# Key and value pages grouped by eight, state updates on the full array, own values in the values' bank, and another order of the mLSTM weight tiles

## The chip, the cores and the metric

One core of one Trainium2 chip runs the whole kernel in one launch. The metric is the device time of the execution in microseconds (us), as the median over the runs.

## The reference

One inference step of a two-layer decoder trunk, for a prompt of 256 tokens and for 8 sample sequences of 8 tokens each (320 token columns in all, model width 2048). Layer 0 projects the input and feeds two groups of heads:

- MoBA attention, 8 heads of 128. The prompt attends causally. Each sample sequence has a paged cache of 2048 keys and values (16 pages of 128); per query the three blocks of 256 keys with the largest `q . mean(k)` are kept, and the new keys (the "own" ones) are added.
- mLSTM matrix memory, 4 heads of 256, with a state `C` (256 x 256) per sample and head, read and replaced.

```python
k_mean = jnp.mean(kb.astype(f32), axis=2)
gate = jnp.einsum('bshd,bnhd->bhsn', q.astype(f32), k_mean)
_, idx = lax.top_k(gate, n_sel)
...
o = jnp.einsum('bhqk,bkhd->bhqd', p[..., :ko], v_own.astype(f32))
o = o + jnp.einsum('bhqnk,bhqnkd->bhqd', p[..., ko:].reshape(bsz, nh, nq, n_sel, kb), v_sel.astype(f32))
...
c_new = decay[..., None, None] * c + jnp.einsum('bhsd,bhse->bhde', kc * wk[..., None], vc)
```

Both groups are gated and go through one output projection and a LayerNorm. Layer 1 is a gated short convolution with four input projections of 2048 and one output projection, again with a LayerNorm. All weights are float32.

## The kernel before, in words

Activations stand transposed (channels on partitions, 320 tokens free). Every weight is cut into tiles of 2048 x 128, and each into two halves of 128 x 1024 floats (512 KB): an *item*. To keep float32 accuracy each half is split into a high and a low part, `sh` by ACT and `sl` by DVE (`split`, line 201), and PE makes three products for each 128 rows (`lin_pe`, line 230): 24 matmuls of 320 columns per half. The bank of the result has the name `lin`.

The cache is read whole. It has 256 *page items* of two 256 KB pages each, grouped into four units (`Unit`, line 441) of four sequences and four heads: 32 key items (`k_item`, line 496) and 32 value items (`v_item`, line 585) per unit. A key item is 4 matmuls, a value item 8; each has a 128-row, 32-column part of the array as its tile, so that four run side by side (`kv<-raw,qp` and `kv<-raw,PT` in the profile). Eight key items give two blocks of scores, eight value items one group `g` of a unit.

All items pass through one ring: SP loads item after item, in the order of the list `items`, into 9 buffers `raw` (`RAW`, line 1376; `ahead`, line 1382). The buffer of a page item is free when PE has used it; that of a weight half when it is split, into one of 4 pairs `sh`/`sl` (`HL`). Before each page load SP reads the page's number from the page table (`page`, line 451). In the list, pages and weight halves are mixed evenly (lines 1154 to 1159): 256 page items to 132 weight halves, that is two page items, then one half, and so on. The last four halves (`TAIL`) come behind all pages.

Everything else (softmax, prompt attention, the mLSTM heads, LayerNorm, the new states) is written as generators in four chains A, B, C, E (`Chain`, line 97), of which one step each is set behind every second 128-row group of a weight half and behind each item (`stages`, line 1414), when a planner (`Plan`, line 69) that counts made-up times per engine finds that its inputs are due. `ahead(must, limit)` decides when a weight half is split: at once if its place is below `must`, otherwise when the planner takes it as loaded. `must` is `i + 2`, the item behind the present one.

The parts that the change touches: `softmax` scales the own scores (line 559); `v_out_task` (line 614) makes the own values' product with four matmuls into bank `mA`, copies it with ACT, and adds it to the transposed output; `post_qm`, `post_km`, `post_vm` (lines 741 to 797) take the mLSTM tiles of a head in the order q, k, v, and the head's generator `mlstm_head` (line 816) is queued behind v; there `states(p)` (line 868) reads two of the eight state tiles `cb` with 4 matmuls, once for each of three groups of tokens and once more for the last (`mC<-cb,qw`). The tiles `cb` have 4 buffers, filled by POOL's DMAs. In `new_states` (line 1233), which runs in layer 1, each of 32 state updates is two matmuls with only 32 rows (`mC<-Xl`), one `scalar_tensor_tensor` of DVE (`xr`), and a load and a store of 256 KB on POOL's queue.

Of the kernel before, what the change touches and what calls it, by code (L numbers as in the profile page):

```python
# [53 lines left out]
TAIL = 4  # L54
SLACK = -0.3
# [94 lines left out]
def trunk_kernel(ctx, tc, x_in, kc, vc, pages, cst_in, seg_in, hot_in, small_in, c0_in, n0_in, w_in,  # L150
# [371 lines left out]
    def softmax(u):  # L522
# [36 lines left out]
        dve.tensor_scalar(S[:, 2048:2112], S[:, 2048:2112], u.rinv[:, 0:1], None, op0=OP.mult)  # L559
# [25 lines left out]
    def v_item(u, g, b4, pp):  # L585
        def pre():
            if (g, b4, pp) == (0, 0, 0):
                u.v = kv_bank()
            if (b4, pp) == (0, 0):
                A.until(f"pt{u.n}.{g}")  # L590
            if (g, b4, pp) == (3, 3, 1):
                C.until(f"post{cga[4 * u.half + 3]}")
                B.until(f"v{4 * u.half + 3}")
                A.until(f"po{u.n}")

        def pe(raw, between):
            r = raw.rearrange("p (g f) -> p g f", g=2)
            for n in range(2):
                for j in range(4):
                    mm(u.v[32 * j:32 * j + 32, 128 * b4:128 * b4 + 128],  # L600
                       lhsT=u.PT[g][:, 2 * pp + n, 32 * j:32 * j + 32], rhs=r[:, n, 128 * j:128 * j + 128], tiles=4,
                       start=g == b4 == pp == n == 0, stop=g == 3 and pp == n == 1, skip_group_check=True)
            if b4 == 3 and pp == 1:
                pv_groups[0] += 1

        def post():
            if u.n:
                A.until(f"out{u.n - 1}")
            O = pa_.tile([128, 4, 128], F32, name="O", tag="O")
            act(O, u.v.rearrange("p (b d) -> p b d", b=4), AF.Identity, scale=u.rinv[:, 0:1])  # L610
            A.add_urgent(f"out{u.n}", v_out_task(u, O))
        return Item(v_load(u, b4, 2 * g + pp), pe, post if (g, b4, pp) == (3, 3, 1) else None, pre=pre, split=False)

    def v_out_task(u, O):

        yield
        t = a_bank()
        for j in range(4):
            h = 4 * u.half + j
            mm(t[:, 32 * j:32 * j + 32], lhsT=vs[:, h * 128:h * 128 + 128], rhs=u.PO[:, 32 * j:32 * j + 32],  # L620
               start=True, stop=True)
        yield HOLD
        own = pa_.tile([128, 4, 32], F32, name="u", tag="u")
        act(own, t[:, :128].rearrange("p (j c) -> p j c", j=4), AF.Copy)
        yield
        t = a_bank()
        for b in range(4):
            transpose(t[:, b * 128:b * 128 + 128], O[:, b, :], ident)
        yield HOLD
        o4 = own.rearrange("p j (b q) -> p j b q", b=4)  # L630
        dve.tensor_tensor(o4, _free(t, 0, [[32, 4], [136, 4], [1, 8]]), o4, op=OP.add)
        m = M[:, 4 * u.half:4 * u.half + 4, T + 32 * u.quad:T + 32 * u.quad + 32]
        dve.tensor_tensor(m, m, own, op=OP.mult)
        yield
# [106 lines left out]
    def post_qm(hd, kt):  # L741
        def f(p):
            if kt == 0:
                if hd >= 1:
                    B.until(f"read{hd - 1}")
                qm[hd] = ml.p.tile([128, 2, N], F32, name="qm", tag="qm")
            act(qm[hd][:, kt, :], p, AF.Copy)
        return f

    def post_km(hd, kt):  # L750
        def f(p):
            if kt == 0:
                km[hd] = ml.p.tile([128, 2, N], F32, name="km", tag="km")
                if hd == 0:
                    c_load(4)
            act(km[hd][:, kt, :], p, AF.Copy, scale=1.0 / 16)
            B.add(f"k{hd}.{kt}", k_natural(hd, kt))
# [5 lines left out]
    def c_load(count):  # L763
        for _ in range(count):
            if ml.c_next < BH * NB:
                c = ml.p.tile([128, 512], F32, name="cb", tag="cb", bufs=4)
                nc.gpsimd.dma_start(c, c0_in[ml.c_next // NB, C_ORDER[ml.c_next % NB]])
                ml.cb.append(c)
                ml.c_next += 1
# [20 lines left out]
    def post_vm(hd, kt):  # L790
        def f(p):
# [3 lines left out]
            if kt == 1:  # L795
                B.add(f"mlstm{hd}", mlstm_head(hd))
# [19 lines left out]
    def mlstm_head(hd):  # L816
# [42 lines left out]
        yield HOLD  # L859
        dve.tensor_tensor(dt[:, 0:384], t[:, 0:384], dt[:, 0:384], op=OP.mult)  # L860
# [3 lines left out]
        sm = P2.tile([128, 64], F32, name="sm", tag="sm")  # L864
        dve.memset(sm[:, 32:48], 1.0)
# [12 lines left out]
        for j, (c, n) in enumerate(TOK):  # L878
            states(j)
# [7 lines left out]
            else:  # L887
                yield
# [243 lines left out]
    for step in MLSTM_ORDER:  # L1132
        for n, c in enumerate(take(6 if step[0] == "h" else 4)):
            i = int(step[1])
            if step[0] == "h":
                lh += lin_items(Lin(c, (post_qm, post_km, post_vm)[n // 2](i, n % 2)))
            else:
# [16 lines left out]
    for n, it in enumerate(order):  # L1154
        items.append(it)
        goal = 2 + (free - 2) * (n + 1) // len(order)
# [27 lines left out]
    def to_out_even():  # L1184
# [10 lines left out]
        for u in X2["U"]:  # L1195
            nc.gpsimd.memset(u[:, 0:2], 0.0)
        X2["nc"] = p.tile([128, 16, 18], F32, name="ncv")
# [35 lines left out]
    def new_states():  # L1233


# [17 lines left out]
        for n in range(BH * NB):  # L1253
# [160 lines left out]
    def stages():  # L1414
# [3 lines left out]
        ahead(i + 2, i + AHEAD)  # L1418
        plan.t = t

# [12 lines left out]
    while i < len(items):  # L1433
# [20 lines left out]
        if it.split:  # L1454
            for n in range(g):
                ended[used_up + n] = end
            ahead(i + 2, i + AHEAD)
            used_up += g
        else:
            freed[i] = end  # L1460
            ahead(i + 2, i + AHEAD)
# [153 lines left out]
```

## Time and profile before

| what | value |
| --- | --- |
| median of 3 runs | 1518.67 us (1513.85 to 1520.48) |
| profiled execution | 1513.19 us, span 1511.4 us |
| PE matmuls busy | 1488.2 us, 98% of the span |
| DVE, ACT, POOL busy | 777.3 us, 593.2 us, 140.8 us |
| TensorE clock, mean granted | 0.996 |
| data moved | 356 MB, mean 236 GB/s |

The span is the time from the first to the last instruction; 1.8 us of the execution lie outside it. Matmuls are pipelined, so that the busy share of PE says little by itself: two neighbours overlap, and what one costs is the distance between their starts. The pages are used from 44 us to 768 us, layer 0's output projection follows until about 905 us, then layer 1.

### The profile page before, as it was taken

Reading aid. Unit: us, or ns where it says so; the run is one execution under the profiler, and the core shown is the slowest. Engines: PE = TensorE matmul, PEld = TensorE weight load, DVE = VectorE, ACT = ScalarE, POOL = GpSimd, SP = SyncE. Lnnn points to the kernel's source line nnn. Section 1 sums busy time; section 2 is a strip of 40 time slices with the busy share of each in tenths; the row PEclk is TensorE's granted clock in tenths of the full one; section 3 lists DMA queues with packets and bytes.
Section 4 is the critical chain, followed back from the end, with each engine's and each line's share of the span. In section 5 each row is a group of like instructions: output and inputs, shape, how many; then the busy total and the mean of one; then the engine's idle time right before and its main releaser. Section 6 shows DMA issues by size and latency. Waiting matters only on the chain.

```text
span 1511.4 us, 31909 instructions
## 1 busy us (share of the span) xinstructions
PE 1488.2 (98%) x11983; PEld 1370.5 (91%) x11983; DVE 777.3 (51%) x1304; ACT 593.2 (39%) x1097; POOL 140.8 (9%) x263
## 2 busy tenths in 40 slices
PE   9999999999999999999999999999999999999998
PEld 9887889988888788899899999999999999999997
DVE  5224334333343423623456766666666666666665
ACT  5224435433334333433354444333333333333444
POOL 0100000010111101101001015313110000000000
PEclk9999999999999999999999999999999999999999
DMA  9999889989989789989864557767555444444422
GB/s 337 294 310 308 298 291 322 317 290 324 310 290 294 268 288 316 311 290 304 291 234 160 190 159 218 217 215 223 203 198 184 141 140 162 145 140 158 153 70 70
DMA packets 148652, 356.42 MB, mean 236 GB/s; under 512 B 24325, under 2 KB 30726, under 8 KB 148498
## 3 DMA queue, kind: packets, MB, share of 16 engines
q1 hardware_dynamic: 126338, 317.26, 61.9%
q0 software_dynamic: 22160, 37.13, 8.3%
q8 instruction: 94, 1.54, 0.4%
q14 instruction: 60, 0.49, 0.1%
HBM read 337.31 MB, written 16.98 MB: 234 GB/s over the span
## 4 chain that ended last, share of the span: by engine, by line
PE 81%; issue 8%; DMA 5%; SPq 2%; DVE 2%; ACT 1%; POOL 1%; ACTq 0%; POOLq 0%; DVEq 0%
PE lin L163 69%; PE kv L163 7%; DMA raw<-w_all 3%; PE mC L163 2%; PE mB L163 2%; DMA bt<-rel 1%; SPq L452 1%; ACT sh L85 1%; PE mB L168 1%; DVE sl L85 1%; DMA cb<-c 0%; SPq L467 0%; PE mA L163 0%; DVE M L85 0%; SPq L459 0%
## 5 line engine op out<-in xcount | busy, mean ns | idle before, releaser
L85 DVE TENSOR_TENSOR sl<-raw,sh 128x1024 fp32r<-128x1024 f32 (+1 forms) x341 | 412.6, 1215 | 527.1 <-ACT sh L85 525.9
L85 ACT ACTIVATE sh<-raw 128x1024 fp32r<-128x1024 f32 (+1 forms) x341 | 355.8, 1048 | 475.9 <-DMA raw<-w_all 255.4
L163 PE MATMUL lin<-Xh,sh 128*128 128x320 f32 x1648 | 532.7, 323 | 1.8 <-DVE sg L85 1.8
L163 PE MATMUL lin<-Xh,sl 128*128 128x320 f32 x1648 | 510.0, 309 | 0.0
L163 PE MATMUL lin<-Xl,sh 128*128 128x320 f32 x1648 | 509.8, 309 | 0.0
L163 PEld LDWEIGHTS lin<-Xh,sh 128*128 128x128 f32 x1648 | 310.5, 188 | 42.3 <-issue 31.3
L163 PE MATMUL lin<-X2h,sh 128*128 128x322 f32 x1024 | 321.9, 314 | 0.0
L163 PE MATMUL lin<-X2l,sh 128*128 128x322 f32 x1024 | 318.0, 311 | 0.0
L163 PE MATMUL lin<-X2h,sl 128*128 128x322 f32 x1024 | 317.8, 310 | 0.0
L163 PEld LDWEIGHTS lin<-Xl,sh 128*128 128x128 f32 x1648 | 311.0, 189 | 0.6
L163 PEld LDWEIGHTS lin<-Xh,sl 128*128 128x128 f32 x1648 | 310.3, 188 | 0.0
L163 PEld LDWEIGHTS lin<-X2h,sh 128*128 128x128 f32 x1024 | 192.9, 188 | 4.4
L163 PEld LDWEIGHTS lin<-X2l,sh 128*128 128x128 f32 x1024 | 193.7, 189 | 0.1
L163 PEld LDWEIGHTS lin<-X2h,sl 128*128 128x128 f32 x1024 | 192.6, 188 | 0.0
L163 PE MATMUL kv<-raw,qp 128*32 128x256 f32 x1024 | 71.0, 388 | 6.2 <-ACT vstage L85 3.3
L163 PE MATMUL kv<-raw,PT 128*32 128x128 f32 x2048 | 71.1, 277 | 0.0
L163 PEld LDWEIGHTS kv<-raw,PT 128*32 128x32 f32 x2048 | 51.8, 110 | 14.1 <-issue 11.8
L163 PEld LDWEIGHTS kv<-raw,qp 128*32 128x32 f32 x1024 | 26.3, 109 | 29.5 <-issue 15.1
L85 DVE SCALAR_TENSOR_TENSOR xr<-xr,dec,mC 128x512 f32<-128x512 f32 x32 | 23.9, 746 | 36.6 <-PE mC L163 31.7
L85 ACT ACTIVATE sg<-sg 128x320 f32<-128x320 f32 x72 | 33.8, 469 | 14.2 <-DVE sg L85 12.5
L85 ACT ACTIVATE lnq<-M 128x320 f32<-128x320 f32 x30 | 14.2, 472 | 59.0 <-DVE M L85 59.0
L85 DVE SCALAR_TENSOR_TENSOR z<-lnc,ze,lin 128x320 f32<-128x320 f32 x64 | 34.7, 542 | 2.9 <-ACT ze L85 2.9
(308 smaller groups left out, 1021.5 us busy)
## 6 DMA issues: line engine op xcount, KB each, us to landing
raw<-w_all SPq DMA_DIRECT2D x335, 512.0 KB, 4.7
raw<-kc SPq DMA_DIRECT2D x256, 256.0 KB, 4.3
raw<-vc SPq DMA_DIRECT2D x256, 256.0 KB, 4.5
cb<-c POOLq DMA_DIRECT2D x32, 256.0 KB, 5.8
xr<-c POOLq DMA_DIRECT2D x32, 256.0 KB, 4.8
cs_o<-xr POOLq DMA_DIRECT2D x32, 256.0 KB, 2.8
xr<-x_in POOLq DMA_DIRECT2D x16, 160.0 KB, 3.4
y_o<-M SPq DMA_DIRECT2D x16, 160.0 KB, 1.8
```

The source lines that it names most:

```text
L85: return fn(out, *a, **k)
L163: nc.tensor.matmul(out, lhsT=lhsT, rhs=rhs, **k)
L168: nc.tensor.transpose(out, in_, identity)
L452: return nc.sync.value_load(pt[0:1, b * NPG + j:b * NPG + j + 1], min_val=0, max_val=NPOOL - 1)
```

## The change

Six edits and a small one, the core of the diff below.

1. `BUNCH = 8`: the list `items` takes eight page items in a row, then the four (sometimes five) weight halves that belong to them.
2. `soon()` replaces `i + 2` as the place below which halves are split at once: it looks ahead over items worth 4 us in the planner's counting (3.5 for a half, 0.5 for a page item). `c_load` adds 0.77 to the planner's DMA time for each tile.
3. `new_states`: ACT copies a block of 128 rows of keys times a column that is 1 in the 32 rows of the sample and 0 elsewhere (tile `kb`), and the two matmuls then have all 128 rows.
4. Own values: four matmuls with 64 rows, 32 columns and 512 elements (`kv<-vs,PO`) add them in the bank of the values, behind the last page of a unit; the four matmuls into `mA`, the copy, one addition and the scaling in `softmax` go.
5. The mLSTM tiles come in the order v, k, q; `mlstm_head` is queued behind q, and the wait for the reads of the head before is at k.
6. In `mlstm_head`, `states(0)` and `states(1)` stand together, and `states(2)` and `states(3)`.
7. A `memset` of DVE moves ahead of two operations.

```diff
-        dve.tensor_scalar(S[:, 2048:2112], S[:, 2048:2112], u.rinv[:, 0:1], None, op0=OP.mult)
...
+            if (g, b4, pp) == (3, 3, 1):
+                for j in range(4):
+                    h = 4 * u.half + j
+                    mm(u.v[32 * j:32 * j + 32, :], lhsT=u.PO[:, 32 * j:32 * j + 32],
+                       rhs=vs[:, None, h * 128:h * 128 + 128].to_broadcast([64, 4, 128]), tiles=4,
+                       start=False, stop=True, skip_group_check=True)
...
-        for j in range(4):
-            h = 4 * u.half + j
-            mm(t[:, 32 * j:32 * j + 32], lhsT=vs[:, h * 128:h * 128 + 128], rhs=u.PO[:, 32 * j:32 * j + 32],
-               start=True, stop=True)
-        yield HOLD
-        own = pa_.tile([128, 4, 32], F32, name="u", tag="u")
-        act(own, t[:, :128].rearrange("p (j c) -> p j c", j=4), AF.Copy)
...
     def post_km(hd, kt):
         def f(p):
             if kt == 0:
+                if hd >= 1:
+                    B.until(f"read{hd - 1}")
...
+                plan.dma += 0.77
...
         for j, (c, n) in enumerate(TOK):
-            states(j)
+            if j == 0:
+                states(0)
+                states(1)
...
-                yield
+                states(2)
                 states(3)
...
+            c = take(6)
+            for n in (4, 5, 2, 3, 0, 1):
+                lh += lin_items(Lin(c[n], (post_qm, post_km, post_vm)[n // 2](i, n % 2)))
...
-    for n, it in enumerate(order):
-        items.append(it)
-        goal = 2 + (free - 2) * (n + 1) // len(order)
+    for n in range(0, len(order), BUNCH):
+        items += order[n:n + BUNCH]
+        goal = 2 + (free - 2) * (n + BUNCH) // len(order)
...
-            for _ in range(6):
+            for _ in range(2):
                 yield
             kS, vS = kv[hd]
-            r = slice(32 * (b % 4), 32 * (b % 4) + 32)
+            kb = late.tile([128, DK], F32R, name="kb", tag="kb")
+            act(kb, kS[:, b // 4, :].bitcast(F32), AF.Identity, scale=X2["rows"][:, b % 4:b % 4 + 1])
+            yield
+            yield
             u = c_bank()
             for kt in range(2):
-                mm(u[:, kt * 256:kt * 256 + 256], lhsT=kS[r, b // 4, kt * 128:kt * 128 + 128], rhs=vS[r, b // 4, :],
+                mm(u[:, kt * 256:kt * 256 + 256], lhsT=kb[:, kt * 128:kt * 128 + 128], rhs=vS[:, b // 4, :],
                    start=True, stop=True)
...
+    def soon():
+
+        n, t = i + 1, 0.0
+        while n < len(items) and t < 4.0:
+            t += 3.5 if items[n].split else 0.5
+            n += 1
+        return n
...
-            ahead(i + 2, i + AHEAD)
+            ahead(soon(), i + AHEAD)
```

What stands on the engines differs at three places. The line numbers of the change are one higher there.

PE, before, at the first key pages of unit 0 (the three `lin` names are the three products of a weight half, of which 24 stand between two visits of the pages):

```order
L163 MATMUL lin<-Xl,sh 128x320
L163 MATMUL lin<-Xh,sl 128x320
L163 MATMUL kv<-raw,qp_102 32x256 x8
L163 MATMUL lin<-Xh,sh 128x320
L163 MATMUL lin<-Xl,sh 128x320
```

PE, with the change, at the same place (96 `lin` matmuls stand between two such visits):

```order
L164 MATMUL lin<-Xl,sh 128x320
L164 MATMUL lin<-Xh,sl 128x320
L164 MATMUL kv<-raw,qp_102 32x256 x32
L164 MATMUL lin<-Xh,sh 128x320
L164 MATMUL lin<-Xl,sh 128x320
```

Eight matmuls (two page items) became 32 (eight items). Over the whole order, matmuls of pages stand in 143 unbroken runs before and in 52 with the change: 32 bunches, and 20 places where a chain's matmuls fall into one.

SP, before, at the loads for unit 0 (each page load has a read of the page table, `TENSOR_LOAD pt`, and two register instructions ahead of it; four of them stand between two loads of weight halves, `raw<-w_all`):

```order
L459 DMA raw<-kc 128x512
L225 DMA raw<-w_all 128x1024
L452 TENSOR_LOAD pt
L452 ISA x2
L459 ISA
L459 DMA raw<-kc 128x512
```

SP, with the change, at the same place (16 page loads stand between two such groups):

```order
L460 DMA raw<-kc 128x512
L226 DMA raw<-w_all 128x1024 x4
L453 TENSOR_LOAD pt
L453 ISA x2
L460 ISA
L460 DMA raw<-kc 128x512
```

Four weight halves are now loaded in a row, behind sixteen page loads with their reads of the page table; their number is the same.

PE, before, at the reads of the old states in mLSTM head 0 (the first of four such visits):

```order
L163 MATMUL lin<-Xh,sl 128x320
L163 MATMUL mC<-cb,qw 32x256 x4
L163 MATMUL mB<-vn,dt 128x257
L163 MATMUL lin<-Xh,sh 128x320
L163 MATMUL lin<-Xl,sh 128x320
```

PE, with the change, at the same place (the first of two visits):

```order
L164 MATMUL lin<-Xh,sl 128x320
L164 MATMUL mC<-cb,qw 32x256 x8
L164 MATMUL mB<-vn,dt 128x257
L169 MATMUL mA<-cst,S 128x128 x4
L164 MATMUL lin<-Xh,sh 128x320
```

All four buffers of `cb` are read at once, and the second visit, 42 to 54 `lin` matmuls later, needs all four filled anew.

## Rows read from the trace of the kernel before

**Rows 1.** The page, parts 1 and 2 (40 slices of 37.8 us).
```profile
PE 1488.2 (98%) x11983; PEld 1370.5 (91%) x11983; DVE 777.3 (51%) x1304; ACT 593.2 (39%) x1097; POOL 140.8 (9%) x263
...
PEclk9999999999999999999999999999999999999999
DMA  9999889989989789989864557767555444444422
GB/s 337 294 310 308 298 291 322 317 290 324 310 290 294 268 288 316 311 290 304 291 234 160 190 159 218 217 215 223 203 198 184 141 140 162 145 140 158 153 70 70
```

**Rows 2.** Busy time by stretch: all pages; then three stretches behind them.
```profile
core 0: us, PE busy (x) PEld busy (x) DVE busy (x) ACT busy (x) POOL busy (x), PEclk, DMA share, GB/s
44.00:768.00 724.00, 710.46 (x6830) 607.41 (x6823) 267.37 (x527) 274.92 (x576) 58.29 (x109) 0.99 0.90 302
768.00:905.00 137.00, 135.22 (x916) 133.99 (x914) 91.05 (x143) 64.94 (x105) 12.96 (x25) 1.00 0.52 176
905.00:1152.00 247.00, 247.00 (x1596) 236.35 (x1594) 165.20 (x247) 89.16 (x154) 66.86 (x120) 1.00 0.66 210
1152.00:1499.00 347.00, 346.96 (x2340) 345.80 (x2340) 221.39 (x336) 134.31 (x222) 1.08 (x2) 1.00 0.39 130
```

**Rows 3.** Timeline of PE around two key page items (start us, us, engine).
```profile
309.61 0.31 PE L163 MATMUL lin<-Xh,sh 128*128 128x320 f32 x1
...
310.34 0.31 PE L163 MATMUL lin<-Xh,sl 128*128 128x320 f32 x1
310.58 1.07 PE L163 MATMUL kv<-raw,qp 128*32 128x256 f32 x16
311.58 0.42 PE L163 MATMUL lin<-Xh,sh 128*128 128x320 f32 x1
311.84 0.31 PE L163 MATMUL lin<-Xl,sh 128*128 128x320 f32 x1
```

**Rows 4.** The same around a single key page item.
```profile
383.77 0.31 PE L163 MATMUL lin<-Xh,sl 128*128 128x320 f32 x1
384.01 0.64 PE L163 MATMUL kv<-raw,qp 128*32 128x256 f32 x8
...
384.84 0.31 PE L163 MATMUL lin<-Xl,sh 128*128 128x320 f32 x1
```

**Rows 5.** Timeline of SP's queue.
```profile
370.47 0.37 SPq L225 DMA_DIRECT2D raw<-w_all  x1
371.68 3.69 SPq L467 DMA_DIRECT2D raw<-vc  x4
375.47 0.37 SPq L225 DMA_DIRECT2D raw<-w_all  x1
```

**Rows 6.** DMA issues: median us to landing, first of 44 to 110 us.
```profile
raw<-w_all SPq DMA_DIRECT2D x13, 512.0 KB, 5.3
```

**Rows 7.** The same of 850 to 1400 us.
```profile
raw<-w_all SPq DMA_DIRECT2D x148, 512.0 KB, 3.9
xr<-c POOLq DMA_DIRECT2D x32, 256.0 KB, 4.8
cs_o<-xr POOLq DMA_DIRECT2D x32, 256.0 KB, 2.8
```

**Rows 8.** Timeline of ACT and DVE: one weight half is split.
```profile
106.16 1.06 ACT L85 ACTIVATE sh<-raw 128x1024 fp32r<-128x1024 f32 x1 [2.33 <-DMA raw<-w_all]
...
107.25 1.23 DVE L85 TENSOR_TENSOR sl<-raw,sh 128x1024 fp32r<-128x1024 f32 x1 [2.66 <-ACT sh L85]
```

**Rows 9.** Timeline of PE around one state update.
```profile
926.69 0.31 PE L163 MATMUL lin<-X2h,sl 128*128 128x322 f32 x1
926.93 0.50 PE L163 MATMUL mC<-Xl 32*128 32x256 f32 x2
...
927.62 0.31 PE L163 MATMUL lin<-X2l,sh 128*128 128x322 f32 x1
```

**Rows 10.** Timeline of PE: from full-array products to full-array transposes.
```profile
300.37 0.31 PE L163 MATMUL lin<-Xh,sl 128*128 128x320 f32 x1
300.51 0.49 PE L168 MATMUL mB<-cst,pS 128*128 128x128 f32 x3
```

**Rows 11.** Timeline of PE around a unit's own values.
```profile
772.78 0.31 PE L163 MATMUL lin<-Xh,sl 128*128 128x320 f32 x1
773.02 1.07 PE L163 MATMUL mA<-PO,vs 64*128 64x32 f32 x8
...
774.27 0.30 PE L163 MATMUL lin<-Xl,sh 128*128 128x320 f32 x1
```

**Rows 12.** The chain of waits at a read of the old states.
```profile
619.14 7.07 DMA cb<-c
```

**Rows 13.** PE around a wait, and granted clock of the stretches around it.
```profile
485.80 0.31 PE L163 MATMUL lin<-Xh,sl 128*128 128x320 f32 x1
488.65 1.08 PE L163 MATMUL kv<-raw,qp 128*32 128x256 f32 x8 [2.54 <-DVE qp L85]
...
484.00:488.00 4.00, 2.11 (x15) 1.84 (x13) 1.69 (x7) 2.39 (x9) 0.00 (x0) 1.00 0.99 340
488.00:492.00 4.00, 3.35 (x18) 2.54 (x19) 1.18 (x4) 1.32 (x4) 0.00 (x0) 0.57 0.74 255
```

More of the change, by code (lines that the diff above doesn't have):

```diff
@@ L54 @@
 TAIL = 4
+BUNCH = 8
 SLACK = -0.3
@@ L601, in pe @@
                        lhsT=u.PT[g][:, 2 * pp + n, 32 * j:32 * j + 32], rhs=r[:, n, 128 * j:128 * j + 128], tiles=4,
-                       start=g == b4 == pp == n == 0, stop=g == 3 and pp == n == 1, skip_group_check=True)
+                       start=g == b4 == pp == n == 0, stop=False, skip_group_check=True)
+            if (g, b4, pp) == (3, 3, 1):
[4 more added lines that the diff above has]
+                       start=False, stop=True, skip_group_check=True)
             if b4 == 3 and pp == 1:
@@ L617, in v_out_task @@
         t = a_bank()
-        for j in range(4):
-            h = 4 * u.half + j
-            mm(t[:, 32 * j:32 * j + 32], lhsT=vs[:, h * 128:h * 128 + 128], rhs=u.PO[:, 32 * j:32 * j + 32],
-               start=True, stop=True)
-        yield HOLD
-        own = pa_.tile([128, 4, 32], F32, name="u", tag="u")
-        act(own, t[:, :128].rearrange("p (j c) -> p j c", j=4), AF.Copy)
-        yield
-        t = a_bank()
         for b in range(4):
@@ L629, in v_out_task @@
         yield HOLD
[L630 to L633, printed above, removed]
+        m = M[:, 4 * u.half:4 * u.half + 4, T + 32 * u.quad:T + 32 * u.quad + 32].rearrange("p j (b q) -> p j b q", b=4)
+        dve.tensor_tensor(m, _free(t, 0, [[32, 4], [136, 4], [1, 8]]), m, op=OP.mult)
         yield
@@ L743, in f @@
             if kt == 0:
-                if hd >= 1:
-                    B.until(f"read{hd - 1}")
                 qm[hd] = ml.p.tile([128, 2, N], F32, name="qm", tag="qm")
             act(qm[hd][:, kt, :], p, AF.Copy)
+            if kt == 1:
+                B.add(f"mlstm{hd}", mlstm_head(hd))
         return f
@@ L794, in f @@
             B.add(f"v{hd}.{kt}", vm_natural(hd, v, kt))
-            if kt == 1:
-                B.add(f"mlstm{hd}", mlstm_head(hd))
         return f
@@ L859, in mlstm_head @@
         yield HOLD
+        sm = P2.tile([128, 64], F32, name="sm", tag="sm")
+        dve.memset(sm[:, 32:48], 1.0)
         dve.tensor_tensor(dt[:, 0:384], t[:, 0:384], dt[:, 0:384], op=OP.mult)
@@ L863, in mlstm_head @@
         hn = P2.tile([128, 3, DK], F32, name="hn", tag="hn")
-        sm = P2.tile([128, 64], F32, name="sm", tag="sm")
-        dve.memset(sm[:, 32:48], 1.0)
         s_ = c_bank()
@@ L887, in mlstm_head @@
             else:
-                yield
+                states(2)
                 states(3)
@@ L1132, in trunk_kernel @@
     for step in MLSTM_ORDER:
[L1133 to L1137, printed above, removed]
+        i = int(step[1])
+        if step[0] == "h":
+            c = take(6)
+            for n in (4, 5, 2, 3, 0, 1):
+                lh += lin_items(Lin(c[n], (post_qm, post_km, post_vm)[n // 2](i, n % 2)))
+        else:
+            for n, c in enumerate(take(4)):
                 lh += lin_items(Lin(c, (post_om, post_gm)[n % 2](2 * i + n // 2, c)))
@@ L1196, in to_out_even @@
             nc.gpsimd.memset(u[:, 0:2], 0.0)
+        X2["rows"] = p.tile([128, 4], F32, name="rows")
+        nc.gpsimd.memset(X2["rows"], 0.0)
+        for i in range(4):
+            nc.gpsimd.memset(X2["rows"][32 * i:32 * i + 32, i:i + 1], 1.0)
         X2["nc"] = p.tile([128, 16, 18], F32, name="ncv")
@@ L1456, in trunk_kernel @@
                 ended[used_up + n] = end
-            ahead(i + 2, i + AHEAD)
+            ahead(soon(), i + AHEAD)
             used_up += g
@@ L1460, in trunk_kernel @@
             freed[i] = end
-            ahead(i + 2, i + AHEAD)
+            ahead(soon(), i + AHEAD)
         pending += [(items[i + n].post, end) for n in range(g) if items[i + n].post]
```

## Prediction

> **What bounds the kernel now.** I read the page first: PE is busy 98% of the span, no slice is below 8 tenths, the granted clock stands at 9 tenths or more in every slice, and the transfers fall from about 300 GB/s to 200 and less behind slice 20 [rows 1]. Busy time by stretch then cuts the span in two kinds of work. While pages are used (44 to 768 us) the DMA share is 0.90, behind them 0.39 to 0.66 [rows 2]. So behind the pages PE alone sets the time; among the pages PE and the loads are close together, and one has to ask of each stretch which of them would end last.
>
> What PE's time consists of is read from the distance between starts. Products follow each other every 0.146 us (five steps from 309.61 to 310.34) [rows 3], so a weight half of 24 takes 3.50. A visit to two page items costs 311.84 - 310.34 less two such steps, 1.21 us [rows 3]; a visit to one item costs 0.78 [rows 4]. The second item adds 0.43, and 0.35 is the price of the visit itself: the turn to the column tiles and back. The 724 us of the pages are then 132 x 3.50 = 462 for weights, 128 x 1.21 = 155 for pages, and 107 for chains and idle time, which is 3.3 per eight page items. One such cycle (8 page items, 4.125 halves) now takes 724 / 32 = 22.6 us.
>
> SP is the second bound. Four page loads and a weight load take it 375.47 - 370.47 = 5.00 us without a wait [rows 5], because each page load has its reads of the table ahead of it: (3.69 - 0.37) / 3 = 1.11 us per load. Four of these are 20.0 of the 22.6 us.
>
> **The change part by part.**
>
> *Bunches on PE.* A bunch of eight costs 0.78 + 7 x 0.43 = 3.79, four visits cost 4.84. By the order there are 52 runs of page matmuls instead of 143: 91 x 0.35 = 32 us of PE time less. A cycle without waits would last 3.79 + 14.4 + 3.3 = 21.5 us.
>
> *Bunches on the loads.* All of the 9 buffers are filled by one bunch and the first half behind it (W1). The second half (W2) goes into the buffer of the bunch's first page item, so SP stands still until PE begins the bunch. Count from that moment. W2 is issued at 0.5, W4 at 1.4 (a weight load follows 0.43 behind its forerunner [rows 5]), the next page load 1.21 later at 2.6, the sixteenth at 2.6 + 15 x 1.11 = 19.3, the next W1 at 19.7. It lands 3.9 later if transfers don't queue [rows 7], 5.3 if they do [rows 6], and is split in 107.25 + 1.23 - 106.16 = 2.3 us [rows 8], of which the first two products hide 0.3. So it is ready 25.6 to 27.0 us after the bunch before began; I take the middle, 26.3. The bunch itself begins 14.4 + 3.3 us after its forerunner's W1. Two cycles are therefore 26.3 + 14.4 + 3.3 = 44.0, one is 22.0: longer than PE's 21.5, and what remains of the gain is 32 x (22.6 - 22.0) = 19 us. PE idles at W1, and chain work counts only half, since it runs while the load is under way. W2 is late too: issued at 0.5, it is ready at 6.4 to 7.8, and PE gets there at 3.79 + 3.50 = 7.3; I take 0.25 per bunch, 8 us. Twenty chain visits inside bunches, five more than before, cost 5 x 0.35 = 2. Sum for the page stretch: **-9 us**. Bounds: with the 2.8 us of a 256 KB store [rows 7] for the landing, W1 never holds PE, -32; with 27.0 and 0.5 for W2 it is -8 + 16 + 2 = +10.
>
> *New states.* An update costs PE 927.62 - 926.69 less two steps, 0.64 us [rows 9]; its two matmuls of 256 columns, at the pace of the products (0.147 for 322), would take 0.23. A turn from products to other full-array matmuls shows no gap: 300.51 - 300.37 = 0.14 [rows 10]. I take 0.41 x 32 = **-13 us**, undiluted, because PE is busy for all of 905 to 1152 us [rows 2]. The 32 copies of ACT are hidden (ACT is busy 89 of 247 us). The updates now have 6.8 us between them on average (46.5 products in the order), once only 4.4; a load (4.8) and a store (2.8) [rows 7] have three buffers and so three times that. If that cover went, DVE would wait in `xr`, and the splits behind it. Bounds: 0 if the 0.64 belongs to the matmuls and not to the turn, -13 otherwise.
>
> The Trainium skill (TensorE: Matmul & The Clock Gate, section Why this matters for your kernels) speaks against this edit: "K=32 single mm = same time as K=128; gain is tile concurrency". By it alone the sum would lose the 13 us; rows 9 and 10 put the cost into the turn, which that sentence leaves open.
>
> *Own values.* A visit costs 774.27 - 772.78 less two steps, 1.20 [rows 11]; the four new matmuls stream 512 elements side by side, twice a page item's 256, so 0.86, in a bunch that is there anyway: 4 x -0.34 = -1.4. The copy, addition and scaling that go were beside the path.
>
> *Old states.* Eight visits less, 8 x -0.35 = -2.8. But four tiles are now read at once, and their four successors are wanted 42 products, some 7 us, later. One such load took 7.07 us on the chain of waits [rows 12]. I take 1 us per head, +4; bounds 0 and +12.
>
> *Tiles v, k, q; `soon()`; the planner's 0.77; the memset.* They move ACT and DVE work within a head or a bunch, beside PE's products; I cost them at nothing. If v and k are not natural in time, `until` at k forces a head's steps out, and PE waits some 2 us in each of three heads: bounds -4 and +6.
>
> **Sum**: -9 - 13 - 1.4 - 2.8 + 4 = -22 us. Against the profiled execution, 1513.2, that is 1491. The three runs lie on average 4.5 us above that execution and their median 5.5, so I forecast **1496 us**, with 1486 to 1506 as this case's own range.
>
> **The rivals.**
>
> *A: the loads keep up.* If W1 is ready by 25 us, PE gets its whole 32 us: -32 - 13 - 4 = -49, 1464, shown as 1469. For it: transfers land in 2.8 to 3.9 us when nothing queues, and in a run of page loads SP issues only 256 KB per 1.11 us, less than the 300 GB/s of the page. Against it: SP has 1.5 us to spare in 21.5, and it stands still at every bunch. Chance 0.25.
>
> *B: the loads take all of it back.* At +10 for the pages, 1513.2 + 10 - 13 = 1510, shown as 1515 to 1518. It needs landings of 5.3 us, which is what 44 to 110 us show [rows 6]. Chance 0.17.
>
> *C: the update's 0.64 us does not fall* with 128 rows: 1509. Chance 0.06.
>
> *D: slower, by the clock.* A wait of PE at 485.80 of 2.85 us was followed by a stretch at a granted clock of 0.57, that is, mostly at the lower level, 1.2 GHz [rows 13]; it cost 4 x 0.43 = 1.7 us. W1 is a place where PE waits in every bunch: in stretches without chain work a cycle is near 21.2, and with 27.0 the idle time there is 27.0 - 21.2 - 3.8 = 2.0 us. If it passes some 2.5 us, the halves behind each bunch run at the lower clock, a cycle grows by half of 1.7, and the change gives +10 - 13 + 14 to 27 = +11 to +24: 1528 to 1542. Against it: waits of that length were rare before, and the mean clock is 0.99 there [rows 2]. Chance 0.09. The Trainium skill (same page, section Loop structure matters more than you think) warns of just this form, a transfer awaited ahead of each run of matmuls; by it D would be the rule rather than the exception.
>
> **How the numbers follow.** My forecast gets 0.43, A 0.25, B 0.17, C 0.06, D 0.09. A change of 0.5% (7.6 us) is about what a measurement of this kernel can tell from none: faster means under 1511, slower over 1526. Faster is my case, A and half of C, 0.71; same is B and the rest of C, 0.19 without B's upper end; slower is D and that end, 0.10. The range takes in A, my case, C and most of B: 1467 to 1522; D and the fringes of A and B stay out.
>
> **What would show it.** In the profile after: page matmuls in groups of 64 records (keys) or 128 (values) in some 3.8 us; the first product behind a bunch waiting 1 to 2 us on `sl` of a half whose transfer came last (right), or following without a gap (A), or with granted clocks of 0.6 behind it in many bunches (D). SP's first wait in a cycle should be a weight load that waits for `kv`. The pages should last about 715 us, the state updates 0.23 us each. The forecast is wrong if the page stretch is under 700 or over 735 us, or the updates stay above 0.5.

## The result, and the profile after

| | before | after |
| --- | --- | --- |
| median (4 runs each, taken together) | 1519.58 us (1513.85 to 1521.06) | 1567.38 us (1565.23 to 1575.84) |
| profiled execution, span | 1513.19, 1511.4 us | 1565.23, 1563.5 us |

The ratio is 1.0332, 95% interval 1.0283 to 1.0381: **slower** by 48 us. The forecast, 1496 us with a range to 1522, was wrong, and in its sign.

The page of the kernel after, part 1 (before: [rows 1]):

```profile
PE 1475.3 (94%) x11983; PEld 1392.4 (89%) x11983; DVE 775.0 (50%) x1296; ACT 599.7 (38%) x1125; POOL 141.3 (9%) x268
```

Busy time by stretch after, its columns as in [rows 2]: pages, and the stretch of the state updates.

```profile
48.00:809.00 761.00, 690.37 (x6723) 613.85 (x6717) 257.15 (x508) 260.33 (x555) 57.57 (x108) 0.96 0.83 280
...
961.00:1208.00 247.00, 243.00 (x1633) 241.87 (x1632) 169.74 (x254) 103.15 (x190) 69.50 (x125) 0.99 0.66 215
```

The loss is in the first stretch: 761 us for the pages against 724 [rows 2], with the DMA share down from 0.90 to 0.83 and the granted clock from 0.99 to 0.96. The two are not quite alike: 8 page items go with 4.125 halves, so with bunches of eight four halves that stood ahead of the last pages now stand behind them (3144 `lin` matmuls between the first and the last page matmul before, 3048 after). With these 4 x 3.5 us the pages cost 775, **51 us more**. They also begin 4 us later (47.6 us against 43.7), and behind them after needs 3 us less (1563.5 - 809 - 14 = 740.5 against 1511.4 - 768 = 743.4). Together that is the 52 us between the two profiled executions.

What PE waited for in the page stretch of after, longest total first (us in total, times, longest us). The same view of before has nine rows, 13.7 us together.

```profile
PE lin L164 <- ACT sh L86: 16.0, 12, 2.5
PE lin L164 <- DVE sl L86: 12.1, 15, 3.3
PE kv L164 <- DVE qp L86: 8.6, 2, 7.2
PE mB L169 <- DVE vms L86: 6.8, 1, 6.8
PE kv L164 <- DMA raw<-vc: 6.1, 5, 2.8
PE mB L169 <- ACT M L86: 5.7, 3, 2.3
PE kv L164 <- DMA raw<-kc: 4.9, 4, 2.0
PE mB L169 <- DVE M L86: 4.3, 1, 4.3
PE mB L169 <- ACT vstage L86: 3.7, 1, 3.7
PE mB L169 <- DVE dec L86: 2.3, 1, 2.3
```

These ten rows add up to 70.5 us: 28.1 at the splits of halves (`sh`, `sl`), 11.0 for pages that landed late, and 31.4 for other work of ACT and DVE (`qp`, `vms`, `M`, `vstage`, `dec`). So the 51 us are, roughly: PE's saving of 32 (91 x 0.35), 70.5 - 13.7 = 57 us of new waits, and the clock: 0.04 x 761 less 0.01 x 724, 23 us. -32 + 57 + 23 = 48. The clock's share does not count the waits twice: over stretches of 4 us, PE's busy time alone times the missing share of the clock is 27.7 us after and 4.4 before, again 23.

**One late cycle.** PE around the bunch at 359.63 and the next (start us, us), then SP's queue, ACT and DVE:

```profile
359.63 0.64 PE L164 MATMUL kv<-raw,qp 128*32 128x256 f32 x8
360.20 0.92 PE L164 MATMUL mC<-kT,M 128*128 128x128 f32 x4
...
383.00 3.66 PE L164 MATMUL kv<-raw,qp 128*32 128x256 f32 x64
388.37 0.42 PE L164 MATMUL lin<-Xh,sh 128*128 128x320 f32 x1 [1.70 <-ACT sh L86]
...
389.63 0.42 PE L164 MATMUL lin<-Xh,sl 128*128 128x320 f32 x1 [0.70 <-DVE sl L86]
```

```profile
360.08 3.04 SPq L226 DMA_DIRECT2D raw<-w_all  x4
363.98 18.00 SPq L460 DMA_DIRECT2D raw<-kc  x16
382.07 2.92 SPq L226 DMA_DIRECT2D raw<-w_all  x4
```

```profile
387.26 1.06 ACT L86 ACTIVATE sh<-raw 128x1024 fp32r<-128x1024 f32 x1 [6.62 <-DMA raw<-w_all]
...
388.35 1.23 DVE L86 TENSOR_TENSOR sl<-raw,sh 128x1024 fp32r<-128x1024 f32 x1 [7.19 <-ACT sh L86]
```

SP is still at W1 when the bunch begins. W4 needs the buffer of the bunch's third item, which chain steps inside the bunch (the first at 360.20) delay; the first page load goes out at 363.98, 4.4 us after the bunch began, W1 22.4 after, and it is split at 389.58, **30.0 us** after. The next bunch began 23.4 after, so PE waits behind it, twice. Over the 31 cycles of the trace the medians are 3.3 us, 21.4 and **29.2**; the earliest W1 was ready after 27.3. In the whole page stretch what SP waits for most (its view of waits, columns as above) is, as forecast, the buffer of a page item, for a weight load:

```profile
SPq L226 <- PE kv L164: 99.2, 61, 10.0
```

The chain of waits of 355 to 392 us agrees: 31.5% of it lie on SP's page loads and table reads, 29% on the transfer of a half, 16% on PE's products.

**Parked work.** PE and, below, ACT and DVE around the longest wait but one:

```profile
505.04 3.26 PE L164 MATMUL kv<-raw,PT 128*32 128x128 f32 x112
515.11 0.90 PE L169 MATMUL mB<-cst,km 128*128 128x128 f32 x3 [6.81 <-DVE vms L86]
```

```profile
512.54 1.06 ACT L86 ACTIVATE sh<-raw 128x1024 fp32r<-128x1024 f32 x1 [10.54 <-DMA raw<-w_all]
...
513.82 0.26 ACT L86 ACTIVATE vms<-mB 64x128 fp32r<-64x128 f32 x1
...
514.77 0.28 DVE L86 TENSOR_TENSOR vms<-mB,vms 64x128 fp32r<-64x128 f32 x1
```

PE stops inside a bunch for a transpose that needs a bank which ACT and DVE have to empty. Both could have done so long before, but `vms` stands in their order behind the split of W1, and ACT stands at that split for 10.5 us. The other waits for `qp`, `vms`, `M`, `vstage` and `dec` look alike in the timelines of ACT and DVE: ahead of each stands a split of a half. A late W1 holds whatever small work is queued behind its split. What that adds to W1's own wait can't be read here: where PE waited inside a bunch for such work, it waited less or not at all behind it.

**The clock.** Busy time by stretch around that wait, and two neighbouring products behind it:

```profile
512.00:516.00 4.00, 0.90 (x7) 0.52 (x11) 1.42 (x2) 1.97 (x5) 1.20 (x3) 0.66 1.03 404
516.00:520.00 4.00, 4.00 (x31) 1.92 (x31) 2.11 (x2) 2.81 (x6) 0.95 (x2) 0.50 1.07 339
```

```profile
522.12 0.47 PE L164 MATMUL lin<-Xh,sh 128*128 128x320 f32 x1
522.39 0.47 PE L164 MATMUL lin<-Xl,sh 128*128 128x320 f32 x1
```

At a granted clock of 0.50, the lower level of 1.2 GHz, a product takes 0.27 us instead of 0.146. Cut into stretches of 4 us, the page stretch has 20 with a clock under 0.8 out of 191; before it had 3 out of 181.

**What came as forecast.** A bunch without waits, and a state update:

```profile
565.13 0.31 PE L164 MATMUL lin<-Xh,sl 128*128 128x320 f32 x1
565.37 3.66 PE L164 MATMUL kv<-raw,qp 128*32 128x256 f32 x64
568.96 0.41 PE L164 MATMUL lin<-Xh,sh 128*128 128x320 f32 x1
569.21 0.31 PE L164 MATMUL lin<-Xl,sh 128*128 128x320 f32 x1
```

```profile
1002.91 0.32 PE L164 MATMUL lin<-X2h,sl 128*128 128x322 f32 x1
1003.07 0.40 PE L164 MATMUL mC<-Xl,kb 128*128 128x256 f32 x2
...
1003.45 0.32 PE L164 MATMUL lin<-X2l,sh 128*128 128x322 f32 x1
```

Less two steps of 0.146 each, the bunch takes 569.21 - 565.13 - 0.29 = 3.79 us, to the digit what was said, and the update 1003.45 - 1002.91 - 0.29 = 0.25, against 0.64 [rows 9].

### The profile page after: what moved, and what is told of

Its sections match the earlier page's. It is cut to its first block, busy times and chain, and to the rows that moved or that the text cites. A ratio compares the mean times of both kernels' runs of the same rounds, so it can differ in the third digit from the quotient of the medians.

```text
span 1563.5 us, 31963 instructions
## 1 busy us (share of the span) xinstructions
PE 1475.3 (94%) x11983; PEld 1392.4 (89%) x11983; DVE 775.0 (50%) x1296; ACT 599.7 (38%) x1125; POOL 141.3 (9%) x268
## 4 chain that ended last, share of the span: by engine, by line
PE 72%; DMA 8%; SPq 7%; issue 7%; DVE 3%; ACT 2%; POOL 1%; ACTq 0%; DVEq 0%; POOLq 0%
PE lin L164 63%; DMA raw<-w_all 6%; PE kv L164 4%; SPq L453 4%; SPq L460 2%; PE mC L164 2%; SPq L468 2%; ACT sh L86 1%; DVE sl L86 1%; PE mB L164 1%; DMA xr<-c 1%; PE mA L169 1%; PE mB L169 1%; POOL Xl L1246 1%; DVE M L86 1%
## 5 line engine op out<-in xcount | busy, mean ns | idle before, releaser
L164 PE MATMUL lin<-Xh,sl 128*128 128x320 f32 x1648 | 519.3, 315 | 12.1 <-DVE sl L86 12.1
L164 PE MATMUL lin<-Xl,sh 128*128 128x320 f32 x1648 | 518.0, 314 | 0.4 <-DVE Xl L86 0.4
L164 PEld LDWEIGHTS lin<-Xh,sh 128*128 128x128 f32 x1648 | 317.7, 193 | 31.0 <-ACT sh L86 20.7
L164 PEld LDWEIGHTS lin<-Xh,sl 128*128 128x128 f32 x1648 | 317.2, 193 | 16.9 <-DVE sl L86 16.7
L164 PEld LDWEIGHTS lin<-Xl,sh 128*128 128x128 f32 x1648 | 317.6, 193 | 1.3 <-DVE Xl L86 0.7
L164 PE MATMUL kv<-raw,qp 128*32 128x256 f32 x1024 | 63.7, 392 | 17.3 <-DVE qp L86 8.6
L164 PE MATMUL kv<-raw,PT 128*32 128x128 f32 x2048 | 63.2, 276 | 6.1 <-DMA raw<-vc 6.1
L164 PEld LDWEIGHTS kv<-raw,qp 128*32 128x32 f32 x1024 | 31.2, 112 | 41.7 <-issue 12.6
```

Source lines behind the costliest of these rows:

```text
L164: nc.tensor.matmul(out, lhsT=lhsT, rhs=rhs, **k)
```

## The experiments

Ratios are to the kernel before, run on the same chip, with a 95% interval; medians differ between chips (before's own from 1511 to 1520 us). "Pairs" are bunches of two.

### Which edit loses: the bunches

`e1`: after with `BUNCH = 2`.

> The changed kernel with bunches of two page items instead of eight; everything else of the change stays. If bunches of eight are what costs the time (by late loads, or by ACT and DVE parked on a late weight half): the page stretch falls from some 780 us to 715 to 725 and the whole to 1495 to 1508. If the other edits (v, k, q order, the earlier splits) cost it: the page stretch stays above 750 and the whole above 1530.

Measured: 1501.87 us, ratio 0.9922 [0.9892, 0.9952]; pages 718 us at clock 0.99.

`e2`: before, with bunches of eight alone:

```diff
-    for n, it in enumerate(order):
-        items.append(it)
-        goal = 2 + (free - 2) * (n + 1) // len(order)
+    for n in range(0, len(order), 8):
+        items += order[n:n + 8]
+        goal = 2 + (free - 2) * (n + 8) // len(order)
```

> The kernel before with bunches of eight alone; splits forced one item ahead as before, 32-row updates, q, k, v. If bunches alone do it: page stretch 760 to 785, whole 1555 to 1580. If the loss needs the earlier forced splits too (ACT and DVE parked on them): page stretch 725 to 745, whole 1515 to 1535. If it comes from the new order of the mLSTM tiles: whole near 1500.

Measured: 1589.98 us, 1.0513 [1.0439, 1.0587]; pages 778 us at clock 0.94. Bunches alone do it, and lose more than the 1580 expected at most.

`e3`: after with `ahead(i + 2, ...)` in place of `ahead(soon(), ...)`. Here, and in `e5`, the steps fall so that head 0's values overwrite a scratch row of `M` that holds the gates' terms for the samples; the samples' mLSTM decays and key weights are then other numbers, the instructions are the same.

> The changed kernel with splits forced only for the next item (as before) instead of 4 us ahead. Theory 'parked engines' (the split of the half behind a bunch stands early in ACT's and DVE's order, waits there for its landing and holds up work that the bunch's own matmuls need): PE's waits inside bunches on qp, vms and bank copies fall, whole 1530 to 1550. Theory 'late loads' alone (the ring of 9 lets that half be loaded too late, whoever waits): no change or up to 15 us slower, 1563 to 1580.

Measured: 1570.88 us, 1.0387 [1.0320, 1.0453]: `soon()` changes nothing that can be told. Parked work stays with it: PE waits 5.8 us for `qp`, 6.1 for `vms` and 8.9 for `M`.

`e5`: after with `BUNCH = 4`.

> The changed kernel with bunches of four in place of eight, all else as in the change. Theory L (the loss is the first half behind a bunch, which SP issues behind all page loads of the bunch): behind eight page loads it is issued about 9 us earlier in its cycle than behind sixteen, so PE rarely waits on it; page stretch 700 to 725 us, time 1480 to 1505, fewer than 20 idle gaps over 0.6 us there. Rival N (a bunch costs in proportion to its length, whatever the loads do: delayed chain steps, column tiles in long runs): a third of the way from bunches of two (1502) to bunches of eight (1567), about 1520 to 1530.

Measured: 1517.71 us, 0.9993 [0.9966, 1.0020]; pages 725 us. Neither theory's number: between the two, just under N's.

What follows: bunches alone cost 79 us on the kernel before (1590 against 1511), all other edits together bring 9 to 12 with pairs (1511 to 1502, or 0.0078) and some 27 with bunches of eight (0.018 between `e2` and after), and the loss grows with the length of the bunch.

### Whose pace: SP's reads of the page table

`e4`: after with page numbers fixed when the kernel is built (`return b * NPG + j` in `page`); its pages are not those of the table.

> The changed kernel with page numbers fixed at build time (page j of sequence b is number 16 b + j), so SP reads no page table: it leaves out the lookup, and its output is of other pages. The same bytes move. 'Late loads' by SP's pace: a page load falls from 1.11 us to some 0.4 on SP, transfers then limit (512 KB per 1.5 us), the half behind a bunch lands 3 to 6 us earlier, page stretch 700 to 730, whole 1485 to 1515. If the waits don't come from the loads' pace: page stretch above 760, whole above 1545.

Measured: 1487.10 us, 0.9833 [0.9771, 0.9895]: the loss is gone and a gain is there. A run of sixteen page loads now takes 10.4 to 15.5 us in place of 17 to 19 (the shortest is the one at 307.36).

`e8`: the same with pairs.

> Bunches of two with page numbers fixed when the kernel is built, so SP reads no table (the output is the reference's only where the table has those pages; instructions of the other engines are the same). If long bunches gain on PE by themselves (91 visits of 0.35 us, 32 us) once the loads keep up, this is slower than bunches of eight with fixed pages (1487) by 10 to 30 us: 1495 to 1515, and SP's reads cost bunches of two nothing. If the reads cost bunches of two their 20 us of idle time too and long bunches gain nothing net, it is 1475 to 1487.

Measured: 1494.44 us, 0.9853 [0.9791, 0.9916]. Bunches of eight are 3 us (by the ratios) to 7 us (by the medians) ahead, less than the 10 to 30 awaited. Two runs of each, with intervals of 9 us to either side, can't tell that from none, nor surely the 7 to 10 us that pairs gain without reads.

`e6`, `e7`: after, and after with pairs, with layer 0's halves issued by POOL (`nc.gpsimd` for `nc.sync` in `lin_load`).

> The changed kernel, bunches of eight, with the weight halves of the first layer issued by POOL's queue; SP keeps the page loads alone. Theory L: a first half then goes out when its buffer is free (when the last half before the bunch has been split), some 15 us before PE wants it; page stretch 690 to 715 us, low clock under 35 us in all, time 1485 to 1510. Rival N: nothing but the queue changes, so 1550 to 1570. A third way: SP still needs 17.8 us for sixteen page loads and the ring is full of weights, so pages come late instead: the waits move from the splits to the page matmuls, 1520 to 1550.

> The same with bunches of two. Theory L: at two the loads are late only now and then (8 gaps, 20.6 us of idle time over 0.6 us), so the second queue brings at most those 20 us: 1482 to 1500. Rival: POOL's queue holds the weights back behind loads of old states that wait for a buffer, and it is slower than 1502.

Measured: 1544.70 us, 1.0184 [1.0087, 1.0282], and 1506.65, 0.9936 [0.9908, 0.9965]. `e6` lies in the third way's range, but its largest waits stayed at the splits (23.9 us, against 10.6 for late pages); `e7` is on the rival's side. `e6` is no clean test: POOL's queue is in order too, and halves stand behind stores whose data isn't there yet. POOL's waits in its page stretch:

```profile
POOL raw L226 <- DVE sl L86: 253.6, 25, 17.1
...
POOL v_o L364 <- ACT vstage L86: 61.5, 6, 16.2
```

`e9`, `e10`, `e11`: eight numbers by one read, in after, in after with pairs, and in before:

```diff
-        return nc.sync.value_load(pt[0:1, b * NPG + j:b * NPG + j + 1], min_val=0, max_val=NPOOL - 1)
...
+        if (b, j) == (b0, j0):
+            at = pt.rearrange("o (b j) -> o b j", b=NB)[:, b0:b0 + nb, j0:j0 + nj]
+            got = nc.values_load_multi_w_load_instructions(at, [mybir.EngineType.SP], min_val=0, max_val=NPOOL - 1)[1]
...
```

> The changed kernel, bunches of eight, with SP reading eight page numbers by one table read (64 reads in place of 512; the two checks of each number and the address step stay). Theory S (the loads are lost to SP's pace: what it stands still behind a bunch it can't make up at 1.11 us per page load): the pace falls to between 0.70 us, which the runs of sixteen loads with fixed pages show (10.44 / 15), and 0.9; page stretch 690 to 725 us, time 1485 to 1525. Rival R (it is the checks and address steps that take the time, not the read, or the pages' transfers themselves): pace above 1.0, 1550 to 1570.

> The same reading with bunches of two. Theory S: pairs have 18.5 us of idle time over 0.6 us in the page stretch, of which fixed pages took away 12 (1502 to 1494); this gives 1492 to 1500, and it is no faster than bunches of eight with the same reading by more than 10 us. Rival R: 1500 to 1504, no change.

> The kernel before with SP reading eight page numbers at a time, nothing else. Theory S: pairs are hardly bound by SP (16 us of idle time over 0.6 us): 5 to 12 us less than before. Rival R: no change within 4 us.

Measured: 1544.28 us, 1.0182 [1.0093, 1.0271]; 1506.20, 0.9914 [0.9887, 0.9942]; 1518.46, 0.9998 [0.9972, 1.0023]. With pairs, reading by eight brings nothing (R's side for both). With bunches of eight the pace fell as theory S said ((12.47 - 0.33) / 15 = 0.81 us a load below), but only a third of the loss against `e1` came back; neither theory's range holds 1544. SP's queue in `e9` around a bunch that began at 90.3:

```profile
91.01 1.29 SPq L226 DMA_DIRECT2D raw<-w_all  x3
96.70 12.47 SPq L468 DMA_DIRECT2D raw<-kc  x16
109.27 1.82 SPq L226 DMA_DIRECT2D raw<-w_all  x4
```

The read (1.73 us at 92.3) and the checks of eight numbers stand between W4 and the first page load: 4.4 us in which nothing is issued. The pace of a run was the wrong measure; what counts is the time from the bunch's begin to W1, 19.0 us here (109.27 less 90.3).

### The reads taken out of the way

`e12`: after; SP reads the next bunch's numbers behind W1's load, where it stands still for the ring anyway. `e13`: the same on before with bunches alone.

```diff
+                if EARLY and items[n_load].split and items[n_load - 1].split and not items[n_load - 2].split:
+                    nxt = [it for it in items[n_load:n_load + BUNCH + 8] if not it.split][:BUNCH]
+                    for it in nxt[::4]:
+                        it.load.read()
                 items[n_load].load(raws[n_load])
```

> The changed kernel, bunches of eight; SP reads the sixteen page numbers of the next bunch (two table reads of eight) right behind W1's load, where it stands still for the ring anyway, and issues the pages' loads without a read between them. In the trace of the run with reads of eight, such a read takes 1.73 us and its checks 8 x 0.26 = 2.1, and a page load 0.55 to 0.58; so two reads take 7.7 us of SP's stand-still, and sixteen page loads 16 x 0.56 = 9.0 us instead of 13 (reads of eight on the spot) or 17.7 (the change). Theory S (SP's time between a bunch's begin and W1 decides): W1 is issued some 11 us after the bunch began, as early as with fixed pages, page stretch 680 to 700 us, time 1475 to 1495. Rival R (the ring of nine, filled by eight pages and W1, stops the transfers at every bunch, whatever SP does; fixed pages were fast for other reasons): 1515 to 1545.

> The kernel before with bunches of eight and the same early reading, without the other edits. Theory S: what bunches alone lost (1590 against 1511) goes, and 10 to 25 us of the gain of 32 on PE stay against before: 1490 to 1510. If the other edits are what let bunches of eight go well (splits forced four microseconds ahead, and tiles in the order v, k, q), it stays over 1530.

Measured: 1509.21 us, 0.9940 [0.9917, 0.9962]; 1529.75, 1.0082 [1.0052, 1.0111]. No page, buffer or wait was changed, and by the ratios 60 of after's 62 us against `e1` came back (65 of 78 with bunches alone): most of the loss is SP's time behind the bunch, not the ring by itself. (A larger ring was not tried.) But `e12` stays 16 to 22 us above fixed pages, below R's range and above S's: W1 went out 16 us after the bunch began, not 11. And `e13` lies above before, at the 1530 where its other theory began: without the other edits part of the loss stays.

`e14`: `e12` with one read of sixteen numbers and without their checks (1.03 us a read, where two reads of eight and their checks were reckoned at 7.7). `e15`: `e14`, and the copies of q for the next unit's keys (`k_start`) recorded one bunch earlier.

```diff
+    def early_start(u):
+        it = order[order.index(segs["K", u.n][0]) - BUNCH]
+        old = it.pre
+        it.pre = lambda: (old and old(), k_start(u))
...
```

> As the run with early reads, but one table read of sixteen numbers per bunch and no check of each number. Early reads still held SP 7.7 us behind W1, and in the first cycles it came to W2 only 2 to 3 us after the bunch had begun (61 reads of eight at a median of 0.68 us, 8 x 0.165 + gaps for the checks). Without the checks a read is 1 to 3 us and SP is free when the bunch begins. Theory S: page stretch 685 to 700 us, time 1480 to 1498, with fixed pages' 1487 in it. If the rest (1509 against 1487) is not SP's reading: 1503 to 1512.

> The same, and the four copies of q that each new unit's keys need (ACT and DVE, 2 each) stand one bunch earlier in their engines' order, ahead of the split of W1. In the run with early reads two bunches of keys waited 5.14 us (at 319.63) and 3.23 us (at 502.63) for copies that stood behind the split of a first half whose transfer was awaited. Theory P (work of PE's next step parked in order behind a split that waits): both waits go, 5 to 9 us less than the run without this edit. If something else would have held PE there: no change.

Measured: 1487.17 us, 0.9793 [0.9761, 0.9825], and **1476.90 us, 0.9716 [0.9682, 0.9749]**, faster than both kernels by a clear margin. `e14` is in theory S's range. From after over `e9`, `e12` and `e14` to `e4` W1 goes out 21.4, 19.2, 16.1, 15.4 and 15.2 us after the bunch before began (medians of 31 cycles), and the times fall along with it (1567, 1544, 1509, 1487, 1487); between `e12` and `e14`, 22 us for 0.7, it is not the whole account.

What PE waited for in `e14`'s page stretch, and in `e15`'s (the two largest rows of each):

```profile
PE lin L165 <- DVE sl L87: 8.0, 6, 4.9
PE kv L165 <- DVE qp L87: 7.1, 2, 4.1
```

```profile
PE lin L165 <- DVE sl L87: 6.6, 5, 4.7
PE lin L165 <- ACT sh L87: 5.0, 2, 3.6
```

The waits for `qp` are gone and the time with them: that is parked work shown by an edit that moves nothing else. `e15`'s pages by stretch, DMA at 0.88 and the clock at 0.99 again:

```profile
44.00:721.00 677.00, 662.56 (x6720) 597.23 (x6723) 258.89 (x510) 262.40 (x558) 57.48 (x107) 0.99 0.88 315
```

`e17`: `e15` with pairs (the read stands before the load that needs it).

> The run with one read of sixteen numbers and early copies of q, with bunches of two in place of eight (the reads stand before the page load that first needs them). It asks what bunches of eight are worth once loads and copies don't hold them. If the prediction's term is right (91 visits of 0.35 us, 32 us of PE time), bunches of eight (1477) are ahead by most of it, less some idle time that pairs don't have: this run takes 1490 to 1505. If pairs gain as much from the cheaper reads, it is 1474 to 1482.

Measured: 1495.60 us, 0.9848 [0.9821, 0.9875]. So bunches of eight are worth 0.9716 / 0.9848, 1.3% or 19 us, once little holds them: PE still waits 14.4 us in `e15`'s page stretch, 8.1 in `e17`'s.

### The state updates

`e16`: `e1` with the update as it was (32 rows, no `kb`).

> Bunches of two with the update of the new states as it was (32 rows, no scaled copy, its six steps before the matmuls), all else as in the change. If the prediction's term for the new states is right, it is 8 to 13 us slower than bunches of two (1502 to 1506): 1510 to 1518, with 0.6 us for each of the 32 visits on PE. If the edit is worth nothing, the same time within 3 us.

Measured: 1507.88 us, 0.9925 [0.9904, 0.9946]. Against `e1`'s 0.9922 the ratios, from different chips, can't tell 8 us. The traces can; the stretch that holds all updates, of `e1` and of `e16`:

```profile
905.00:1152.00 247.00, 242.89 (x1649) 242.37 (x1649) 171.09 (x254) 104.28 (x191) 67.31 (x121) 1.00 0.67 215
```

```profile
905.00:1152.00 247.00, 247.00 (x1596) 236.42 (x1595) 165.56 (x247) 87.53 (x152) 64.01 (x116) 1.00 0.66 209
```

In the same 247 us 53 more matmuls: 53 x 0.147 = 7.8 us. The distances between starts agree: less two steps each, the 32 visits together take 20.1 us in `e16` and 12.3 in `e1` (before 20.1, after 12.2). Thirty of them take 0.23 to 0.25, two take 1.4 and 3.6 to 3.8. PE is idle for 4 us; of after's `mC` matmuls the view by tile says what for, and the timelines of DVE and ACT what lay behind the longer wait, which ended at 993.17:

```profile
  ACT kb L86: 4.0, 2
```

```profile
988.46 0.75 DVE L86 SCALAR_TENSOR_TENSOR xr<-xr,dec,mC 128x512 f32<-128x512 f32 x1 [6.91 <-DMA xr<-c]
...
991.00 0.57 ACT L86 ACTIVATE yc<-U,small 128x336 f32<-128x336 f32 x1 [10.71 <-DVE U L86]
...
992.62 0.49 ACT L86 ACTIVATE kb<-Xl,rows 128x256 fp32r<-128x256 f32 x1
```

DVE stood 6.9 us at the load of an old state, ACT stood at `yc` for DVE's `U` behind it, and `kb` stands behind `yc`. The shorter wait was for a load of the keys themselves (`Xl<-kd`).

## Why the prediction was wrong

*What bounds the kernel.* Right as far as it went: PE, with SP close behind. It left out that ACT and DVE, in order, hang on SP too.

*Bunches on PE* (-32). Right: 3.79 us a bunch, and in `e15` against `e17` 19 us of the 32 are left; 6 of the rest are the waits that bunches keep. The 2 us for "twenty chain visits" are counted twice: the 52 runs hold them already. Kernels whose loads nearly keep up come near rival A's 1469, too: 1487 (`e4`, `e14`) and 1477 (`e15`, which also moves the copies of q).

*Bunches on the loads.* **The step that failed.** "The next page load 1.21 later at 2.6", "the next W1 at 19.7", "ready 25.6 to 27.0 us after the bunch before began": the mechanism was right, W1 behind sixteen loads. The sizes weren't: 3.3, 21.4 and 29.2 in the median, 4.4, 22.4 and 30.0 in the cycle shown, and no cycle was as quick as the 27.0 of the upper bound. I let the ring give its buffers back at PE's undisturbed pace, and chain steps inside a bunch hold them; the sixteen loads took 18.0 us and not 17.1; and W1 needed 7.5 us from its issue to the end of its split, not 6.6. Put into the forecast's own sum, 29.2 gives a cycle of (29.2 + 14.4 + 3.3) / 2 = 23.45 us, and the median cycle was 23.5: 27 us lost where the sum kept 19. That is 46 of the some 60 us by which the term missed. Two things that the term left out take part in the rest: work of ACT and DVE parked behind a split that waits (`vms`, `qp`, up to 7.2 us at a time; in `e15` moving the copies of q alone brought 10 us), and the clock, 23 us. How they divide in after, with what the late W1 already holds, was not measured. The forecast's own sign of error, a page stretch over 735 us, was there. The term came out at +51 instead of -9; for the four halves that now stand behind the pages the stretch should have been forecast 14 us shorter than 715.

*New states* (-13). The visit fell to 0.25 as said, "undiluted" was wrong: twice PE waited for `kb`. ACT's share of 89 us in 247 said nothing of its order: in the longer wait the copy stood behind work that hung on a load of an old state, the very wait in `xr` that the forecast named ("If that cover went") and priced at nothing. Net -7.8. Rival C fell. The Trainium skill's sentence (TensorE: Matmul & The Clock Gate, section Why this matters for your kernels) on K=32 leaves out the turn: the visit went from 0.64 to 0.25 us.

*Own values* (-1.4). The four new matmuls last from 282.13 to 283.13 us in `e15`, 1.00 instead of 0.86: still less than the 1.20 of before [rows 11].

```profile
282.13 1.06 PE L165 MATMUL kv<-vs,PO 64*32 64x512 f32 x8
283.13 0.66 PE L170 MATMUL mA<-cst,S 128*128 128x128 f32 x4
```

*Old states; v, k, q; `soon()`; the planner* (+1.2 and 0). Right with pairs, where all edits but the bunches bring 9 to 12 us; 7.8 of them are the updates and some 1 the own values, which leaves 0 to 3. Too low a value with bunches of eight, where they bring 20 (`e12` against `e13`). `soon()` shows no part in it (`e3`); how the other 12 divide between old states and tile order was not tried.

*Rival D* (0.09). Its mechanism came true. Its price for the clock, 14 to 27 us, holds 23; its time, 1528 to 1542, doesn't hold 1567, because D was thought of in place of late loads' other costs and came with them. Its idle time of 2.0 us rests on a cycle of 21.2 that is worked out nowhere; 27.0 and 14.4 over two cycles give 20.7, and 2.5 us of idle time. That waits of this length "were rare before" was no evidence against it, as the change is what makes them. The Trainium skill (same page, section Loop structure matters more than you think) warned of this form, and the 20 stretches under 0.8 agree.

*Rival B* (loads take all back) was bounded at +10 by W1's landing alone; W1 came later than that bound in every cycle, and the clock came on top.

## What to carry to other kernels

Where a queue feeds a ring, ask not for its mean pace but for the time from the moment a buffer comes free to the issue of the load that is wanted first; whatever can be done ahead of that moment (here table reads) belongs ahead of it. On an engine that works in order, a wait for a transfer holds all that is queued behind it: list that work, put what others wait for ahead of the wait, and price a late transfer with it. Longer runs of one kind of work save turns, but they make loads bursty and can add a wait at each end, and long waits can cost a second time in the clock behind them.

## What the runs showed of the hardware

A table read of SP takes 0.27 us for one number (median of 476 in after), 1.03 for sixteen (30 in `e15`), 0.06 a number; reads of eight in `e9` took 0.54 to 2.22, 0.68 in the median:

```profile
L453 SPq TENSOR_LOAD <-pt x476: 262/269/771, 49.1 to 769.0; - x159
```

```profile
L458 SPq TENSOR_LOAD <-pt x30: 1026/1033/1983, 60.0 to 686.4; - x30
```

The checks of a number, 0.15 us and the gaps about it, cost as much as the read. And PE's clock did not fall behind every wait: after the waits of 1.64 and 0.70 us that ended at 366.8 and 368.1 the granted clock stayed at 1.00, after the wait of 6.8 us it was 0.50.
